# Summing the first adaLN gate on VectorE in column order, and holding the second gate's quarters back until the unsplit part of w_gate_up

## The chip, the core and the metric

The kernel runs on one core of a Trainium2 chip. A core has TensorE (PE in the profile; its weight loads are PEld), VectorE (DVE), ScalarE (ACT), GpSimd (POOL) and SyncE (SP), which here only issues the DMAs. The metric is the device time of one execution in microseconds (us). Before the change it is 1233.91 us, the median of three runs (1233.58 to 1235.08). All times below come from these runs or from one profiled execution of the same kernel.

## The reference, cut to what matters

One layer of a block over 256 tokens of width 2048, all in float32. What the change touches is the adaLN modulation: six vectors of 2048 values, made from one conditioning row `c` and a 2048 x 12288 matrix.

```python
mod = einsum('bd,de->be', silu(c), w_ada) + b_ada
shift1, scale1, gate1, shift2, scale2, gate2 = split(mod, 6)
h = rms_norm(x, norm1_w) * (1 + scale1) + shift1
proj = h @ w_in                      # 2048 x 6152
...                                  # mLSTM (4 heads) and differential attention (8 heads)
mix = concatenate([h_ml, o_da]) @ w_out
x = x + gate1 * mix
h = rms_norm(x, norm2_w) * (1 + scale2) + shift2
g, u = split(h @ w_gate_up, 2)       # 2048 x 11264
x = x + gate2 * ((silu(g) * u) @ w_down)
```

`gate1` is first needed when the first output columns of `w_out` are complete, `shift2` and `scale2` when the FFN's input is made, `gate2` only when the first output columns of `w_down` are complete.

## The kernel before

**The big products.** All four weight matrices are streamed once, in chunks of 128 x 1024 values. For each chunk ScalarE makes a rounded high half (`wh`, line 211) and VectorE the rest (`wl`, line 181); the activations exist in the same two halves (`hh`, `hl`, and others). TensorE then makes three products for each pair of column block and token half (lines 569 to 571), twelve products of 128 x 512 for one chunk. One chunk is a *tick*, and the kernel has 392 of them, written out in order by `visit`: the input projection in seven sweeps (ticks 0 to 95), the output projection (96 to 127, "wo"), the first twelve column groups of `w_gate_up` in three sweeps f0, f1, f2 over two, three and three of the eight column pairs of the input (128 to 223), its other ten groups in one piece (224 to 303, "fr"), and `w_down` (304 to 391, "dn"). f0 needs the column pairs 0 and 1 of the second scale and shift, f1 the pairs 2 to 4, f2 the pairs 5 to 7. The last two ticks of "wo" and the first two of f0 are split by token half; this is the turn.

**The modulation.** `w_ada` is loaded in 192 *quarters* of 128 x 1024 values (0.5 MB), eight eighths (p) of four quarters for each of the six vectors (s). The list `items` gives their order: the first scale and shift interleaved (64), the first gate (s = 2, 32), the second scale and shift interleaved (64), the second gate (s = 5, 32). A quarter is summed in one of two ways, told apart by `on_pe(s, p)`, which also picks its layout in memory (`_layout`):

- on TensorE: four matrix products with the activated `c` as weights (line 216; eight instructions in the profile) into a PSUM bank `gv`; after the fourth quarter ScalarE copies the row out (`gr`), TensorE turns it by two transposes into a second bank (`gc`, line 220), ScalarE copies that into `gsum`. A bank is held from the first of the four quarters on.
- on VectorE: one multiply with the activated `c` spread over the partitions (`silc`), with its sum written to `gsum` (line 185; two instructions in the profile).

`modcol` adds the partial sums of `gsum` and the bias on GpSimd (lines 377 and 379). For a gate, `gate_rows` does so once for all 16 columns, when all eight eighths are there, and then makes the gate's row in four pieces: VectorE spreads 512 values on a diagonal (`g1rd` for the first gate), TensorE multiplies by ones (`g1rp`), ScalarE copies. That is thirteen steps, at most one a half tick. `residual` multiplies the output columns by that row.

**What sets the order.** The program is written out half tick by half tick. A `Plan` keeps a running count of the work that waits on VectorE (`plan.v`), ScalarE (`plan.a`) and TensorE (`plan.p`), of the loads' landing times and of four free PSUM banks. In each half tick the loop at the end of `tile_block` emits the halves of the weights for two ticks ahead, then whatever small steps of attention, mLSTM, norm and gates are due (`plan.run`, in the order of a list, and only while `plan.v` and `plan.a` are at most 2.3 us), then the products. When a tick needs something that is not there yet, `plan.until` emits the steps of that alone, without products, until it is there.

Quarters are taken from the list, strictly in order, at two places. `due(i)` is a pace: as many quarters as `ADA_PLAN` has promised by tick i are taken at once, whatever else waits. `ada_idle` takes more when there is room: on TensorE while `plan.p` is at most 0.6 (and, at an eighth's first quarter, two banks are free), on VectorE while `plan.v` is at most 1.8, and only when the load should have landed. The ring of buffers `ada` holds four quarters; `ada_dma` issues the next load on SP's queue each time one is taken. SP issues in order, so a load that waits for its buffer holds up the weight loads behind it. Near the end of fr, the last two of the eleven FFN activation groups are written into the four buffers of this ring (`make_aT`, n of 9 and 10).

Of the kernel before, what the change touches and what calls it, by code (L numbers as in the profile page):

```python
# [27 lines left out]
NADA = 4  # L28
# [7 lines left out]


def on_pe(s, p):
    return (s == 1 and p % 3 != 2) or s == 2 or (s == 0 and p < PE0)


PE0 = 4
# [122 lines left out]
def tile_block(ctx, tc, x, c, pos, par, w_ada, w_in, w_gt, w_out, w_gu, w_dn, out):  # L165
# [85 lines left out]
    def load_x(cb, again=""):  # L251
        xs[cb] = slab(f"x{cb}{again}")
        nc.sync.dma_start(xs[cb].rearrange("p (t n) -> p t n", t=2), x_v[cb])
        plan.load(0.5)
# [45 lines left out]
    items = []  # L300
# [8 lines left out]
    ada_next = [0, 0]  # L309
    ada_ready = []  # L310

    def ada_dma(n=None):
        while ada_next[0] < len(items) and ada_next[0] < ada_next[1] + NADA and (n is None or n > 0):
            s, p, q = items[ada_next[0]]
            t = sl.tile([P, 1024], F32, name=f"ada{s}_{p}_{q}", tag="ada", bufs=NADA)
            nc.sync.dma_start(t[:], w_ada[s, p, q])
            ada_tiles[s, p, q] = t
            ada_ready.append(plan.load(0.5))
            ada_next[0] += 1
            n = None if n is None else n - 1  # L320

    def ada_use():
        s, p, q = items[ada_next[1]]
        t = ada_tiles.pop((s, p, q))
        if on_pe(s, p):
            if q == 0:
                assert plan.free > 0, "no bank"
                plan.free -= 1
                gemv[s, p] = misc(f"gv{s}_{p}")
            pg = gemv[s, p]  # L330
            for j in range(4):
                mm(pg[32 * j:32 * j + 32, :256], scol[:, q * 4 + j, :], t[:, j * 256:(j + 1) * 256], q == 0, q == 3,
                   passes=1.2, tile_position=(0, 32 * j))
            if q == 3:
                def finish():
                    yield 0
                    row = sm.tile([P, 256], F32, name=f"gr{s}_{p}", tag="gr", bufs=1)
                    act(row[:], pg[:, :256], AF.Copy)
                    plan.rel(1)
                    yield 1  # L340
                    pc = misc(f"gc{s}_{p}")
                    for j in range(2):
                        tr(pc[:, j * 128:(j + 1) * 128], row[:, j * 128:(j + 1) * 128])
                    yield 0
                    act(gsum[:, s, :, p * 2:p * 2 + 2],
                        pc[:, :256].rearrange("p (j a b) -> p a j b", j=2, b=32)[:, :, :, 0], AF.Copy)
                    plan.rel(1)
                w = Work(f"ada{s}_{p}", finish(), ())
                w.last = plan.now
                plan.works.insert(0, w)  # L350
        else:
            j, h = p * 2 + q // 2, q % 2
            stt(t[:], t[:], 1.0, silc[h][:], ALU.mult, ALU.mult, accum=gsum[:, s, h, j:j + 1])
            if q == 3:
                plan.mark(f"ada{s}_{p}")
        ada_next[1] += 1
# [152 lines left out]
    def weights_dma(limit=None):  # L509
        while state["dma"] < len(ticks) and state["live"] < NRAW and (limit is None or limit > 0):  # L510
            i = state["dma"]
            t = ticks[i]
            n = chunk_of[i][2]
            raw = wp.tile([P, 2048], F32, name=f"r{i}", tag="raw", bufs=NRAW)
            nc.sync.dma_start(raw[:, :n * 1024], t["src"][t["kb"]][:, t["h"] * 1024:(t["h"] + n) * 1024])
            raws[i] = raw
            raw_ready[i] = plan.load(n / 2)
            state["dma"] += n
            state["live"] += 1
            limit = None if limit is None else limit - 1  # L520

    def weights_hi(i):
        while state["hi"] <= min(i + HI_AHEAD, len(ticks) - 1):
            k = state["hi"]
            first, idx, n = chunk_of[k]
            if first not in raws:
                break
            plan.t = max(plan.t, raw_ready[first] - AHEAD * TICK)
            his[k] = wp.tile([P, 1024], F32R, name=f"wh{k}", tag="hi", bufs=NHL + HI_AHEAD)
            act(his[k][:], raws[first][:, idx * 1024:(idx + 1) * 1024], AF.Copy)  # L530
            state["hi"] += 1

    def weights_lo(i):
        while state["hl"] <= min(i, len(ticks) - 1):
            k = state["hl"]
            first, idx, n = chunk_of[k]
            raw = raws[first]
            hi = his.pop(k)
            lo = wp.tile([P, 1024], F32R, name=f"wl{k}", tag="lo", bufs=NHL)
            tt(lo[:], raw[:, idx * 1024:(idx + 1) * 1024], hi[:].bitcast(F32), ALU.subtract)  # L540
            wtiles[k] = (hi, lo)
            state["hl"] += 1
            if idx == n - 1:
                state["live"] -= 1
                del raws[first]
# [524 lines left out]
    def turn(stage, heads):  # L1070

        if stage == 0:
            residual_half(("wo", 3), rows1, 3, xs[3], 0)
            square_x(1, 3, 0, SQ0)
            finish_rms(1, 0)
            for p in range(2):
                next(heads[p, 0])
        elif stage == 1:
            plan.free -= 2
            for p in range(2):  # L1080
                next(heads[p, 0])
        elif stage == 2:
            residual_half(("wo", 3), rows1, 3, xs[3], 1)
            del accs["wo", 3], apart["wo", 3]
            plan.rel(1)
            next(heads[0, 0], None)
            square_x(1, 3, 1, SQ1)
            next(heads[1, 0], None)
            finish_rms(1, 1)
            for p in range(2):  # L1090
                next(heads[p, 1])
        elif stage == 3:
            plan.free -= 2
            for p in range(2):
                next(heads[p, 1])
        else:
            for p in range(2):
                next(heads[p, 1], None)
            plan.mark("norm2")
# [83 lines left out]
    spans = {}  # L1183
# [8 lines left out]
    for n, (groups, p0, p1) in enumerate(SWEEPS):  # L1192
        a = len(ticks)
# [4 lines left out]
    a = len(ticks)  # L1198
# [13 lines left out]
    for r, (p0, p1) in enumerate(FSWEEPS):  # L1212
        a = len(ticks)
# [10 lines left out]
    a = len(ticks)  # L1224
# [4 lines left out]
    a = len(ticks)  # L1229
# [12 lines left out]
    def load(span, n, margin):  # L1242
        a, b = spans[span]
        loads.append((a, max(b - margin, a + 1), n))

    for key, n, margin in ADA_PLAN:
        load(key, n, margin)

    def due(i):
        n = 8  # L1250
        for a, b, k in loads:
            n += k * min(max(i + 1 - a, 0), b - a) / (b - a)
        return min(int(n + 1e-6), len(items))


    plan.t = 3.2
    ada_dma(4)
    weights_dma(1)
    for cb in range(4):
# [5 lines left out]
    for n in range(4):  # L1265
        ada_use()
        ada_dma(1)
        if n < 3:
            next(h0)
# [68 lines left out]
    for i, t in enumerate(ticks):  # L1338
        plan.next_half()
        if i == turning + 1:  # L1340
            turn(4, heads)
        for fn in pending:
            fn()
        pending = []
        if i in (turning - 1, turning):
            turn((i - turning + 1) * 2, heads)
        weights_hi(i + AHEAD)
        weights_lo(i + (AHEAD if i == 0 or not LO_LATE or t["split"] is not None else AHEAD - 1))
        weights_dma()
        while ada_next[1] < due(i):  # L1350
            ada_use()
            ada_dma(1)
        ada_dma()
        if i == spans["wo"][0]:
            for cb in range(4):
                load_x(cb, "r")
        plan.run()
        if t["split"] is None:
            ada_idle()
        need = list(t["ready"])  # L1360
        if t["done"] and t["acc"][0] == "wo":
            need.append("rows1")
        plan.until(need, lambda: ada_idle(VFORCE))
        products(i, 0)
        plan.next_half()
        if i == turning - 2:
            weights_hi(turning + 1)
            weights_lo(turning + 1)
        elif t["split"] is None:
            weights_lo(i + AHEAD)  # L1370
            plan.run()
            ada_idle()
        products(i, 1)
        if i in (turning - 1, turning):
            turn((i - turning + 1) * 2 + 1, heads)
        pending += [fn for fn in (t["done"], t["mid"]) if fn]
# [17 lines left out]
        return next(self.gen)  # L1394


ADA_PLAN = ((0, 12, 3), (1, 16, 4), (2, 24, 3), (3, 4, 0), (4, 8, 0), (5, 8, 0), ("wo", 16, 22), ("f0", 24, 5), ("f1", 32, 5), ("f2", 32, 8))


def _layout(a):  # L1400
# [68 lines left out]
```

## Time and profile before

| | |
|---|---|
| median of three runs | 1233.91 us |
| the profiled execution | 1233.24 us |
| its span (first to last instruction) | 1231.5 us |
| granted TensorE clock, mean | 0.992 of full |
| quarters on TensorE / on VectorE | 72 / 120 |
| first gate's quarters (`gv` from 214 us on) | 214.9 to 339.7 us |
| quarters on VectorE, first and last | 54.6 and 707.9 us |

A row of a windows answer gives, for one stretch of the span, its length, then the busy time and number of instructions (x) of each engine in it, the granted TensorE clock, the mean busy share of the 16 DMA engines and their GB/s. With a tile's name it counts that tile's instructions alone. A row of a timeline gives start and duration in us, the engine, the line, the operation, the tile written and those read; in brackets the idle time ahead of it and what ended that. The records of consecutive matmuls overlap, since they are pipelined: what one costs is read from start to start.

### The profile page before, as it was taken

How to read it: one execution, taken by the hardware profiler on the slowest of the kernel's cores; microseconds unless marked ns; L12 is line 12 of the kernel's file. 1: busy time of each engine (PE TensorE's matmuls, PEld its weight loads, DVE VectorE, ACT ScalarE, POOL GpSimd, SP SyncE). 2: the span in 40 equal slices, each digit the busy share in tenths (PEclk: the TensorE clock that was granted, in tenths of full speed). 3: DMA queues.
4: the chain of work that ended last, by engine and by line, in shares of the span. 5: the costliest groups of instructions: out<-in, count | busy, mean ns of one | idle time of the engine just before them, and what ended most of it. 6: DMA issues, size and time to landing. Idle time of an engine off the chain costs nothing.

```text
span 1231.5 us, 15419 instructions
## 1 busy us (share of the span) xinstructions
PE 1208.9 (98%) x5842; PEld 956.2 (78%) x5842; DVE 815.3 (66%) x1064; ACT 587.1 (48%) x817; POOL 113.2 (9%) x250
## 2 busy tenths in 40 slices
PE   6999999999999999999999999999999999999998
PEld 2667878666778787788888888888888878888886
DVE  2656977577587998887988977445455454545443
ACT  3654454457566645855434544444444443343342
POOL 1010121210212412101100000000000000000000
PEclk8999999999999999999999999999999999999999
DMA  8879898757676898798999756555545545646471
GB/s 335 303 279 372 327 372 293 294 187 292 206 288 233 320 358 336 265 345 305 350 342 334 274 195 221 200 177 196 184 177 199 201 171 171 222 171 232 160 256 52
DMA packets 63260, 313.84 MB, mean 255 GB/s; under 512 B 6993, under 2 KB 7377, under 8 KB 41169
## 3 DMA queue, kind: packets, MB, share of 16 engines
q1 hardware_dynamic: 63186, 312.86, 70.1%
q8 instruction: 46, 0.75, 0.2%
q14 instruction: 28, 0.23, 0.1%
HBM read 310.73 MB, written 2.10 MB: 254 GB/s over the span
## 4 chain that ended last, share of the span: by engine, by line
PE 96%; DMA 1%; DVE 1%; ACT 1%; issue 0%; SPq 0%; POOL 0%; ACTq 0%
PE gv L216 3%; PE acc('dn', 0)_8036 L571 2%; PE acc('dn', 0)_8036 L569 2%; PE acc('dn', 2)_8838 L571 2%; PE acc('dn', 2)_8838 L570 2%; PE acc('dn', 1)_8458 L571 2%; PE acc('dn', 1)_8458 L570 2%; PE acc('dn', 0)_8036 L570 2%; PE acc('dn', 1)_8458 L569 2%; PE acc('dn', 2)_8838 L569 2%; DMA ada<-in_w_ada_dram 1%; PE apart('dn', 3)_9219 L571 1%; PE apart('dn', 3)_9219 L570 1%; PE acc('dn', 3)_9218 L571 1%; PE acc('dn', 3)_9218 L570 1%; PE apart('dn', 3)_9219 L569 1%
## 5 line engine op out<-in xcount | busy, mean ns | idle before, releaser
L181 DVE TENSOR_TENSOR wl<-r,wh 128x1024 fp32r<-128x1024 f32 x392 | 474.5, 1222 | 254.3 <-ACT wh L211 252.8
L211 ACT ACTIVATE wh<-r 128x1024 fp32r<-128x1024 f32 x392 | 410.3, 1058 | 409.6 <-DMA r<-in_w_gu_dram 62.1
L185 DVE SCALAR_TENSOR_TENSOR ada<-ada,silc 128x1024 f32<-128x1024 f32 x120 | 144.8, 1219 | 0.0
L377 POOL TENSOR_TENSOR modc<-part,gsum 128x2 f32<-128x2 f32 (+1 forms) x34 | 25.4, 747 | 395.1 <-DVE ada L185 277.5
L216 PE MATMUL gv<-ada,early 128*32 128x256 f32 x576 | 46.3, 416 | 4.3 <-DMA ada<-in_w_ada_dram 4.2
L216 PEld LDWEIGHTS gv<-ada,early 128*32 128x32 f32 x576 | 13.4, 112 | 29.4 <-issue 20.0
L569 PE MATMUL acc('dn', 0)_8036<-wh,aTh 128*128 128x512 f32 x88 | 35.9, 408 | 0.0
L379 POOL TENSOR_TENSOR modc<-modc,gsum 128x2 f32<-128x2 f32 (+1 forms) x58 | 30.9, 533 | 46.8 <-DVE ada L185 43.4
L571 PE MATMUL acc('dn', 0)_8036<-wh,aTl 128*128 128x512 f32 x88 | 34.3, 390 | 0.0
L570 PE MATMUL acc('dn', 0)_8036<-wl,aTh 128*128 128x512 f32 x88 | 34.3, 389 | 0.0
L569 PE MATMUL acc('dn', 1)_8458<-wh,aTh 128*128 128x512 f32 x88 | 34.2, 389 | 0.0
L570 PE MATMUL acc('dn', 1)_8458<-wl,aTh 128*128 128x512 f32 x88 | 34.2, 389 | 0.0
L571 PE MATMUL acc('dn', 1)_8458<-wh,aTl 128*128 128x512 f32 x88 | 34.2, 389 | 0.0
L569 PE MATMUL acc('dn', 2)_8838<-wh,aTh 128*128 128x512 f32 x88 | 34.2, 389 | 0.0
L570 PE MATMUL acc('dn', 2)_8838<-wl,aTh 128*128 128x512 f32 x88 | 34.2, 389 | 0.0
L571 PE MATMUL acc('dn', 2)_8838<-wh,aTl 128*128 128x512 f32 x88 | 34.2, 389 | 0.0
L181 DVE TENSOR_TENSOR hl<-hx,hh 128x512 fp32r<-128x512 f32 (+1 forms) x18 | 11.4, 632 | 26.5 <-ACT hh L211 26.2
L211 ACT ACTIVATE hx<-pt,modc,gcol 128x256 f32<-128x256 f32 (+1 forms) x36 | 17.4, 534 | 17.3 <-PE pt L220 11.5
L211 ACT ACTIVATE gr<-gv 128x256 f32<-128x256 f32 x18 | 6.9, 383 | 32.6 <-PE gv L216 32.6
L570 PEld LDWEIGHTS acc('dn', 0)_8036<-wl,aTh 128*128 128x128 f32 x88 | 16.5, 188 | 4.2 <-issue 1.0
L569 PEld LDWEIGHTS acc('dn', 0)_8036<-wh,aTh 128*128 128x128 f32 x88 | 16.5, 188 | 4.2 <-issue 1.0
L211 ACT ACTIVATE aTh<-at 128x512 fp32r<-128x512 f32 x22 | 11.9, 595 | 15.9 <-PE at L220 15.9
(987 smaller groups left out, 3019.0 us busy)
## 6 DMA issues: line engine op xcount, KB each, us to landing
ada<-in_w_ada_dram SPq DMA_DIRECT2D x192, 512.0 KB, 5.7
r<-in_w_gu_dram SPq DMA_DIRECT2D x76, 1024.0 KB, 5.0
r<-in_w_dn_dram SPq DMA_DIRECT2D x44, 1024.0 KB, 4.8
r<-in_w_in_dram SPq DMA_DIRECT2D x36, 1024.0 KB, 6.9
r<-in_w_out_dram SPq DMA_DIRECT2D x16, 1024.0 KB, 7.4
r<-in_w_in_dram SPq DMA_DIRECT2D x24, 512.0 KB, 5.9
r<-in_w_gu_dram SPq DMA_DIRECT2D x24, 512.0 KB, 5.3
x<-in_x_dram SPq DMA_DIRECT2D x4, 512.0 KB, 5.6
```

Of the source, the lines that this page charges most:

```text
L181: nc.vector.tensor_tensor(o, a, b, op=op)
L185: nc.vector.scalar_tensor_tensor(out=o, in0=a, scalar=s, in1=b, op0=op0, op1=op1, accum_out=accum)
L211: nc.scalar.activation(o, a, func, **kw)
L216: nc.tensor.matmul(o, l, r, start=start, stop=stop, **kw)
L377: nc.gpsimd.tensor_tensor(o, parts[0], parts[1], op=ALU.add)
L379: nc.gpsimd.tensor_tensor(o, o, y, op=ALU.add)
L569: nc.tensor.matmul(o, ah[:, s], wh[:, r], start=t["start"] and j == 0, stop=False)
L570: nc.tensor.matmul(o, ah[:, s], wl[:, r], start=False, stop=False)
L571: nc.tensor.matmul(o, al[:, s], wh[:, r], start=False, stop=t["stop"] and j == 1)
```

## The change

- The first gate's quarters are no longer TensorE's: `on_pe` is false for s = 2. They are laid out and summed like those of the second gate, on VectorE.
- No quarter of the second gate is loaded before the unsplit part of `w_gate_up` begins: `ada_dma` stops at `ada_limit`, 160 of the 192, until tick 224. The pace for f2 falls from 32 to 8 quarters, and from the fifth tick of fr on `due` asks for the last 32 in equal steps, up to 24 ticks ahead of its end.

```diff
 def on_pe(s, p):
-    return (s == 1 and p % 3 != 2) or s == 2 or (s == 0 and p < PE0)
+    return (s == 1 and p % 3 != 2) or (s == 0 and p < PE0)
...
+    ada_limit = [len(items) - 32]
+
     def ada_dma(n=None):
-        while ada_next[0] < len(items) and ada_next[0] < ada_next[1] + NADA and (n is None or n > 0):
+        while ada_next[0] < ada_limit[0] and ada_next[0] < ada_next[1] + NADA and (n is None or n > 0):
...
             n += k * min(max(i + 1 - a, 0), b - a) / (b - a)
+        a, b = spans["fr"]
+        if i >= a + 4:
+            n = len(items) - 32 + 32 * (i - 3 - a) / (b - 24 - a)
         return min(int(n + 1e-6), len(items))
...
         weights_dma()
+        if i == spans["fr"][0]:
+            ada_limit[0] = len(items)
+            ada_dma()
         while ada_next[1] < due(i):
...
-ADA_PLAN = (..., ("f1", 32, 5), ("f2", 32, 8))
+ADA_PLAN = (..., ("f1", 32, 5), ("f2", 8, 8))
```

More of the change, by code (lines that the diff above doesn't have):

```diff
@@ L1394, in __next__ @@
         return next(self.gen)
-ADA_PLAN = ((0, 12, 3), (1, 16, 4), (2, 24, 3), (3, 4, 0), (4, 8, 0), (5, 8, 0), ("wo", 16, 22), ("f0", 24, 5), ("f1", 32, 5), ("f2", 32, 8))
+ADA_PLAN = ((0, 12, 3), (1, 16, 4), (2, 24, 3), (3, 4, 0), (4, 8, 0), (5, 8, 0), ("wo", 16, 22), ("f0", 24, 5), ("f1", 32, 5), ("f2", 8, 8))
 def _layout(a):
```

## The prediction

> **What bounds the kernel now.** I read the page first: the span, the engines' totals, the slices and the chain that ended last.
>
> ```profile
> span 1231.5 us, 15419 instructions
> ...
> PE 1208.9 (98%) x5842; PEld 956.2 (78%) x5842; DVE 815.3 (66%) x1064; ACT 587.1 (48%) x817; POOL 113.2 (9%) x250
> ...
> DVE  2656977577587998887988977445455454545443
> ...
> PE 96%; DMA 1%; DVE 1%; ACT 1%; issue 0%; SPq 0%; POOL 0%; ACTq 0%
> ```
>
> The chain that sets the end is TensorE for 96% of its length. VectorE is busy for 66% on the whole, but unevenly: five to nine tenths in the first 23 slices, four to five tenths behind them. So the windows come next, cut where the projections begin: the input projection's last sweeps (206 to 391), the output projection (391 to 487), the three sweeps f0, f1, f2 over the split part of w_gate_up, and (from a second answer) its unsplit part fr.
>
> ```profile
> core 0: us, PE busy (x) PEld busy (x) DVE busy (x) ACT busy (x) POOL busy (x), PEclk, DMA share, GB/s
> 206.00:391.00 185.00, 185.00 (x1105) 137.22 (x1105) 132.65 (x266) 108.84 (x247) 34.23 (x99) 1.00 0.70 249
> 391.00:487.00 96.00, 95.34 (x431) 78.17 (x429) 88.98 (x127) 51.24 (x77) 27.43 (x41) 1.00 0.90 341
> 487.00:559.00 72.00, 69.06 (x313) 56.23 (x312) 57.58 (x80) 48.54 (x69) 7.58 (x12) 1.00 0.82 303
> 559.00:658.00 99.00, 99.00 (x442) 81.97 (x441) 87.14 (x106) 42.65 (x47) 9.97 (x10) 1.00 0.89 329
> 658.00:760.00 102.00, 102.00 (x471) 84.59 (x470) 84.06 (x90) 50.16 (x55) 2.65 (x4) 1.00 0.71 248
> ```
> ```profile
> 760.00:983.00 223.00, 223.00 (x1005) 184.98 (x1005) 109.85 (x96) 93.17 (x95) 0.00 (x0) 1.00 0.55 194
> ```
>
> TensorE has no gap anywhere but at the turn into the FFN (69.06 of 72). Work taken off it shortens its stretch unless something else becomes late; work moved between stretches in which it is never idle changes nothing. VectorE stands at 72% in 206:391, where the first gate is summed, and at 93% (88.98 of 96) right behind.
>
> **What leaves TensorE.** The first gate's 32 quarters are eight TensorE instructions each (`gv`), and each eighth of the gate ends in two transposes (`gc`). What one costs is read from the starts of its neighbours.
>
> ```profile
> 220.09 0.39 PE L570 MATMUL acc('in', 0, 4)_1821<-wl,hh 128*128 128x512 f32 x1
> 220.32 0.39 PE L571 MATMUL acc('in', 0, 4)_1821<-wh,hl 128*128 128x512 f32 x1
> 220.64 0.64 PE L216 MATMUL gv<-ada,early 128*32 128x256 f32 x8
> 221.21 0.50 PE L569 MATMUL acc('in', 0, 4)_1821<-wh,hh 128*128 128x512 f32 x1
> ...
> 233.42 0.40 PE L571 MATMUL acc('in', 2, 4)_1950<-wh,hl 128*128 128x512 f32 x1
> 233.74 1.07 PE L216 MATMUL gv<-ada,early 128*32 128x256 f32 x16
> 234.74 0.50 PE L569 MATMUL acc('in', 2, 4)_1950<-wh,hh 128*128 128x512 f32 x1
> ```
> ```profile
> 227.40 0.40 PE L571 MATMUL acc('in', 2, 4)_1950<-wh,hl 128*128 128x512 f32 x1
> 227.63 0.38 PE L220 MATMUL gc<-ident,gr 128*128 128x128 f32 x2
> 227.77 0.48 PE L569 MATMUL acc('in', 2, 4)_1950<-wh,hh 128*128 128x512 f32 x1
> ```
>
> Two products follow each other by 0.23 us (220.09, 220.32). Around one quarter it is 221.21 - 220.32 = 0.89, so the quarter costs 0.66; a pair costs 234.74 - 233.42 - 0.23 = 1.09; a pair of transposes 0.37 - 0.23 = 0.14, more where it stands alone among other transposes. In the timeline of `gv` half of the 32 stand alone (x8) and half in pairs (x16): 16 x 0.66 + 8 x 1.09 = 19.3, and 8 x 0.14 = 1.1: 20.4 us. The totals of the same tiles bound it from above:
>
> ```profile
> 206.00:391.00 185.00, 18.79 (x256) 5.86 (x256) 3.08 (x8) 1.00 0.70 249
> ```
> ```profile
> 206.00:391.00 185.00, 3.10 (x16) 2.17 (x16) 1.40 (x8) 1.00 0.70 249
> ```
>
> 18.79 + 3.10 = 21.9. I take **21 us** off TensorE, all of it in a stretch where nothing else was late: 206:391 would last 164. ScalarE loses 3.08 and the eight copies behind `gc`; it is at 59% there and not on the path: nothing. The eight banks for `gv` and eight for `gc` come free for attention, which I count at nothing.
>
> The Trainium skill speaks against reading it so: "Perfetto Trace Analysis", Identifying the Most-Contended Engine, says that a busy matmul row is no measure of TensorE's distance to its roofline, and takes the share of weight loads instead. By that rule the page's 78% would leave TensorE slack; the starts above, 0.23 apart without a break, say that in this stretch each instruction taken out closes up.
>
> **What VectorE gets.** One quarter there:
>
> ```profile
> 397.63 1.21 DVE L185 SCALAR_TENSOR_TENSOR ada<-ada,silc 128x1024 f32<-128x1024 f32 x1
> 398.77 0.07 DVE L185 DVE_READ_ACCUMULATOR ada<-ada,silc 128x1 f32 x1
> 398.77 1.21 DVE L185 SCALAR_TENSOR_TENSOR ada<-ada,silc 128x1024 f32<-128x1024 f32 x1
> ```
>
> From start to start 1.14 us, so 32 x 1.14 = 36.5 us. Whether they fit is a budget, and it needs VectorE's quarters of before, stretch by stretch (each is two instructions):
>
> ```profile
> 206.00:391.00 185.00, 11.50 (x20) 1.00 0.70 249
> 391.00:487.00 96.00, 32.53 (x54) 1.00 0.90 341
> 487.00:559.00 72.00, 22.57 (x37) 1.00 0.82 303
> 559.00:658.00 99.00, 34.60 (x58) 1.00 0.89 329
> ```
>
> About 9 quarters were done by 391, all of the second scale and shift; then 27, 18 and 29. Other VectorE work in 206:391 is 132.65 - 11.50 = 121.2. In the shortened 164 us at the 93% of the row behind it there is room for 152.5 - 121.2 = 31.3 us, 27 quarters. So of 41 (32 and those 9) some 14 slip into the output projection. There the rate cannot rise (93%), so the slip stays 14: the gate's last 5 come first, some 18 us in (5 of 27 in 96 us), and 22 of the second scale and shift by the turn, where 16 are needed. f0 was at 80% (57.58 of 72): 0.93 x 72 - 57.58 = 9.4 us, 8 quarters caught up. At f1's first ticks 40 are needed and 9 + 27 + 18 - 14 + 8 = 48 are there; at f2's 64 are needed and all are there. Each need is met, with 6 to 8 quarters to spare.
>
> What is queued behind the added quarters is VectorE's in-order list: the low halves of the weights, which TensorE needs within two ticks, and the steps of attention. The planner lets a quarter in only while its count of waiting VectorE work is at most 1.8 us, and the pace it must keep asks for only 16 of the 32 by the output projection. Two places are tight already.
>
> ```profile
> 397.71 2.53 DVE ada L185 x5
> ...
> 401.14 0.68 DVE odl L185
> ...
> 401.86 0.50 PE acc('wo', 0)_3635 L571
> ```
>
> At the output projection's start attention's last output comes from VectorE behind three quarters, and TensorE waits. If attention ends one tick later (12 products, 12 x 0.23 = 2.7 us) that is paid in full, for little other TensorE work is left there: **+2.7** (bounds 0, where the freed banks make up for it, to four ticks, 11).
>
> The other is the first gate's rows, needed when the first output columns end, 12 ticks (32 us) in:
>
> ```profile
> 348.94 1.19 POOL L377 TENSOR_TENSOR modc<-part,gsum 128x16 f32<-128x16 f32 x1
> 350.22 0.81 POOL L379 TENSOR_TENSOR modc<-modc,gsum 128x16 f32<-128x16 f32 x3
> ```
> ```profile
> L216 PE MATMUL g1rp<-g1rd,ones x8: 592/592/595, 374.8 to 408.7; 128*128 128x512 f32 x8
> L181 DVE TENSOR_TENSOR g1rd<-ident,modc x4: 677/683/684, 367.2 to 403.5; 128x512 f32<-128x512 f32 x4
> ```
>
> Before, the gate was summed by 348.94 and its rows were spread over 367 to 409. Now the last quarter falls 18 us into the stage; 14 us are left for 13 steps, one a half tick (17.7 us). So one or two of the four row pieces are made with TensorE waiting, each 0.68 on VectorE and 0.59 on TensorE: 2 x 1.27 = **+2.5** (bounds 0, and 4 x 1.27 plus GpSimd's 1.19 + 0.81: 7).
>
> **What is moved and costs nothing.** The second gate's 32 quarters leave f0 to f2, where TensorE shows no idle time but the 2.9 us at the turn, so nothing is gained. They land in fr with their 32 transfers of 0.5 MB on SP's queue; each waits there for the sum that frees its buffer, and the weight loads behind it wait too. The cover: VectorE has 109.85 of 223 us in fr, with 36.5 more 66%; the memory traffic was 194 GB/s, and even if the greedy filler takes the 32 in two thirds of fr (16.8 MB in 149 us, 113 GB/s more) that is about 307, below the 329 of 559:658, where 29 quarters went through in 99 us and TensorE was busy for all of them. Nothing, then; without that cover it would be a few us of late weights. The buffers are free again before the two last activations of the FFN, which take them over. The second gate's rows wait for the last activation anyway.
>
> **The sum.** 21 - 2.7 - 2.5 = 15.8. The profiled execution took 1233.24, 1.74 more than its span; so a span of 1215.7 and a run of 1217.4. The median of the three runs is 0.67 above the profiled one: **1218**.
>
> **The rivals.**
>
> A (forecast): as above; bounds of the unknown costs 0 to 18 of the 21.
>
> B: all 36.5 us of sums fit into VectorE's idle time and the freed banks bring attention forward. For it: 185 - 132.65 = 52 us idle in that stretch. Against it: 41 quarters by 391 need 121.2 + 46.7 = 168 of 164. It gives 1233.9 - 21 = 1213, or 1211 with a little at the turn.
>
> C: the slip grows beyond its reserve: the second scale and shift come late at the turn or at f1, and TensorE waits for quarters at 1.14 us each, with a transfer behind each. At 6 to 8 missing it costs 7 to 9 us beyond A's sum: 1226. For it: the reserve is only 6 to 8 quarters and the transfers in f0 and f1 already take 0.82 and 0.89 of the DMA engines. Against it: the reserve is positive at each of the three needs.
>
> D (slower): the quarters push attention's steps back, because its chain runs through the same in-order engine and the planner holds back steps at 2.3 us of waiting VectorE work, a mark that a quarter let in at 1.8 passes at once. From attention's end on TensorE waits in full: eight ticks late (8 x 2.7 = 21.6) use up the gain, nine make it slower. If VectorE keeps 26 of its 52 idle us (waits for TensorE and ScalarE inside the chain) and takes all 41 quarters first, the stretch lasts 132.65 + 36.5 + 26 = 195 instead of 185: 1244. Against it: the pace forces only 16 quarters there, 121.2 + 18.2 = 139 of 164 us.
>
> E: TensorE's freed time is taken up by waits that its dense row hides: no change, 1233. Against it stands the run of products 0.23 apart. It is where the rule of the Trainium skill's "Perfetto Trace Analysis" named above would lead.
>
> F: GpSimd becomes slow, and with it the reciprocal roots in attention.
>
> ```profile
> 368.01 1.06 POOL L389 TENSOR_TENSOR mfb<-mfb,mfx 128x4 f32<-128x4 f32 x1
> ...
> 369.44 0.20 POOL L391 TENSOR_TENSOR mf<-mf,mfb 128x4 f32<-128x4 f32 x1
> ```
>
> The same kind of operation takes 0.20 or 1.06, about one VectorE pass longer. A root is 12 such steps; if each met a quarter, 12 x 0.86 = 10 us would come on top ahead of the output projection, less the 2.7 counted: 1225. The Trainium skill, "SBUF — State Buffer", Who interferes with whom, gives this as a lock: a VectorE instruction with two SBUF inputs, as a quarter is, holds up a GpSimd instruction that reads SBUF. The trace agrees for a few of them; most steps of that root took 0.20 beside a busy VectorE.
>
> That the change does not do what it says: the second gate is not really paced evenly, since the filler takes quarters whenever there is room; it costs nothing either way.
>
> **How the numbers follow.** A 0.62, B 0.10, C 0.09, F 0.04, D 0.10, E 0.05. What a measurement of this kernel can tell from no change is about 0.2%, 2.5 us. A, B, C and F are faster: 0.85; E the same: 0.05; D slower: 0.10. The range 1211 to 1231 takes in A with its bounds (1213 to 1231), C, F and most of B; D, E and B's lower end, about 0.18, are left out.
>
> **What would show it.** No `gv` from 206 on; 152 quarters on VectorE instead of 120; the stretch from the first `acc('in', 0, 4)` to the end of the input projection at about 164 us; VectorE there above 90%; `g1rd` later than the start of the output projection; fr still 223 us with VectorE at two thirds; f0 to f2 unchanged in length. The prediction is wrong if TensorE shows idle time ahead of the output projection that adds up to more than some 10 us, or if a wait for `hh` or `hl` appears at the start of f1, or if fr grows.

## The result, and the profile after

The changed kernel takes 1241.1 us (median of four runs, 1240.32 to 1242.34) where the kernel before takes 1233.88: a ratio of 1.0058, 95% interval 1.004 to 1.0075. It is slower, by 7 us; 16 us of gain were forecast. The page of its profile:

```profile
span 1239.2 us, 14932 instructions
...
PE 1193.1 (96%) x5570; PEld 953.3 (77%) x5570; DVE 849.6 (69%) x1128; ACT 584.2 (47%) x801; POOL 118.4 (10%) x250
...
DVE  2656978799887998878855677878645454545453
...
PEclk8999999999997999999999999999999999999999
...
PE 85%; DVE 7%; POOL 2%; ACT 2%; issue 2%; DMA 1%; SPq 0%; DVEq 0%; ACTq 0%; POOLq 0%
```

TensorE is busy for 16 us less (the 21 us of the change, less some 5 us by which the rest got longer; more of this at the end), and is now 85% of the chain where it was 96%: VectorE, GpSimd and ScalarE have come onto it. In the 13th slice (372 to 403 us) the granted TensorE clock falls to 0.7. The windows, cut at the first product of each stage (last sweeps of the input projection; output projection; f0; fr), first after and then before at the same cuts:

```profile
207.20:365.50 158.30, 153.31 (x768) 124.38 (x767) 138.56 (x264) 94.27 (x189) 32.59 (x82) 0.99 0.63 227
365.50:496.20 130.70, 111.14 (x497) 88.37 (x495) 114.02 (x186) 64.07 (x122) 33.16 (x53) 0.93 0.86 318
496.20:566.70 70.50, 68.39 (x309) 55.99 (x310) 56.70 (x78) 47.11 (x65) 11.12 (x16) 1.00 0.78 289
...
768.40:990.60 222.20, 222.20 (x1002) 184.25 (x1002) 144.61 (x160) 93.20 (x95) 2.59 (x4) 1.00 0.72 269
```
```profile
207.00:391.70 184.70, 184.70 (x1104) 136.98 (x1103) 131.65 (x264) 109.54 (x249) 34.44 (x102) 1.00 0.70 249
391.70:489.80 98.10, 95.66 (x432) 78.02 (x430) 91.06 (x133) 52.09 (x79) 26.97 (x38) 1.00 0.91 345
```

The last sweeps of the input projection take 26.4 us less (158.3 against 184.7), and the output projection takes 32.6 us longer (130.7 against 98.1), with TensorE idle for 19.6 of it. The first is more than the 21 us because steps of attention and of the mLSTM slipped from one into the other: 65 TensorE instructions more than before stand in the output projection (497 against 432). f0 is a microsecond longer; f1, f2, fr and w_down are as long as before. So nearly all of the loss lies in these two stretches, and their sum is the number to follow below: **282.8 us before, 289.0 after, 261.8 if the 21 us had been gained**.

TensorE's waits in the changed kernel's output projection (who waited for whom: total us, times, longest):

```profile
PE ot L220 <- DVE o L181: 7.2, 1, 7.2
PE po L216 <- ACT aTs L211: 5.0, 3, 2.6
PE g1rp L216 <- DVE g1rd L181: 3.0, 1, 3.0
```

They are waits for attention's last heads (`ot`, `po`) and for the first gate's rows (`g1rp`). The chain that ended last, there:

```profile
366.08 2.08 ACT pm L211 x8
...
370.74 0.75 DVE pm L185 x2
371.49 1.14 DVE wl L181
372.62 1.07 DVE st L196 x4
...
373.83 1.06 POOL st L775
...
375.37 1.62 ACT pm L211 x7
...
377.42 0.95 PE po L216 x6
...
383.13 1.12 POOL of L390
...
387.39 1.22 DVE o L181
388.62 2.88 DVE ada L185 x5
...
392.05 0.67 DVE odl L185
392.77 0.79 PE acc('wo', 0)_3293 L573
```

Softmax (ScalarE), combination (`pm`), row maxima (`st`), scaling (GpSimd), softmax again, values, the root of the norm (GpSimd, twelve steps from 383.1 to 387.4), then nearly three microseconds of gate sums ahead of the low half (`odl`) for which the output product at 392.77 waits: one step after another. Beside the first of them TensorE still had output products, the last at 374.1 us; from there to 390.6 it had none, only attention's own small products and transposes. The order in which the program was written out says the same: at the third tick of the output projection, 13 half ticks were forced without products, and 8 more up to the twelfth tick; before there was one.

### The profile page after: what moved, and what is told of

The parts are those of the page before. It is cut to its first block, busy times and chain, and to the rows that moved or that the text cites. A ratio compares the mean times of both kernels' runs of the same rounds, so it can differ in the third digit from the quotient of the medians.

```text
span 1239.2 us, 14932 instructions
## 1 busy us (share of the span) xinstructions
PE 1193.1 (96%) x5570; PEld 953.3 (77%) x5570; DVE 849.6 (69%) x1128; ACT 584.2 (47%) x801; POOL 118.4 (10%) x250
## 4 chain that ended last, share of the span: by engine, by line
PE 85%; DVE 7%; POOL 2%; ACT 2%; issue 2%; DMA 1%; SPq 0%; DVEq 0%; ACTq 0%; POOLq 0%
DVE wl L181 2%; PE gv L216 2%; PE acc('dn', 0)_7884 L573 2%; PE acc('dn', 0)_7884 L572 2%; PE acc('dn', 2)_8686 L572 2%; PE acc('dn', 2)_8686 L571 2%; PE acc('dn', 1)_8306 L572 2%; PE acc('dn', 1)_8306 L571 2%; PE acc('dn', 0)_7884 L571 2%; PE acc('dn', 1)_8306 L573 2%; PE acc('dn', 2)_8686 L573 2%; DVE ada L185 1%; DMA ada<-in_w_ada_dram 1%; PE at L220 1%; PE apart('dn', 3)_9067 L572 1%
## 5 line engine op out<-in xcount | busy, mean ns | idle before, releaser
L185 DVE SCALAR_TENSOR_TENSOR ada<-ada,silc 128x1024 f32<-128x1024 f32 x152 | 183.4, 1219 | 1.0 <-DMA ada<-in_w_ada_dram 1.0
L571 PE MATMUL acc('dn', 0)_7884<-wh,aTh 128*128 128x512 f32 x88 | 35.9, 408 | 0.0
L573 PE MATMUL acc('dn', 0)_7884<-wh,aTl 128*128 128x512 f32 x88 | 34.3, 390 | 0.0
L572 PE MATMUL acc('dn', 0)_7884<-wl,aTh 128*128 128x512 f32 x88 | 34.3, 389 | 0.0
L571 PE MATMUL acc('dn', 1)_8306<-wh,aTh 128*128 128x512 f32 x88 | 34.2, 389 | 0.0
L572 PE MATMUL acc('dn', 1)_8306<-wl,aTh 128*128 128x512 f32 x88 | 34.2, 389 | 0.0
L573 PE MATMUL acc('dn', 1)_8306<-wh,aTl 128*128 128x512 f32 x88 | 34.2, 389 | 0.0
L571 PE MATMUL acc('dn', 2)_8686<-wh,aTh 128*128 128x512 f32 x88 | 34.2, 389 | 0.0
L572 PE MATMUL acc('dn', 2)_8686<-wl,aTh 128*128 128x512 f32 x88 | 34.2, 389 | 0.0
L573 PE MATMUL acc('dn', 2)_8686<-wh,aTl 128*128 128x512 f32 x88 | 34.2, 389 | 0.0
```

Of the source, the lines that this page charges most:

```text
L185: nc.vector.scalar_tensor_tensor(out=o, in0=a, scalar=s, in1=b, op0=op0, op1=op1, accum_out=accum)
L571: nc.tensor.matmul(o, ah[:, s], wh[:, r], start=t["start"] and j == 0, stop=False)
L572: nc.tensor.matmul(o, ah[:, s], wl[:, r], start=False, stop=False)
L573: nc.tensor.matmul(o, al[:, s], wh[:, r], start=False, stop=t["stop"] and j == 1)
```

## The experiments

The theories. **1, order:** without TensorE's quarters the planner's half ticks are shorter, its count of VectorE work decays less in each, and attention's steps are held back at its mark until they stand bare. **2, VectorE's time:** it cannot take 36.5 us more there. **4, the hold** of the second gate costs. **5, the chain:** attention's steps run through five engines and need their time; TensorE's quarters were work beside them, and without them TensorE waits. Theory 5 came up after the first four runs (there was no theory 3). "Stretch" is the sum of the two stretches above, in the profiled execution; "short" sums, products and roots do part of the work and leave the result incomplete or less exact. Each ratio is against the kernel before on the same chip.

| run | us | ratio, 95% interval | stretch |
|---|---|---|---|
| e1 first gate alone | 1244.05 | 1.0075 (1.006 to 1.009) | 288.9 |
| e2 hold alone | 1234.17 | 0.9998 (0.9989 to 1.0008) | 282.9 |
| e3 short sums | 1231.45 | 0.9978 (0.9968 to 0.9988) | 279.5 |
| e4 mark at 3.4 | 1243.35 | 1.0067 (1.0052 to 1.0082) | 289.3 |
| e5 first gate free | 1238.33 | 1.0023 (1.0008 to 1.0038) | 283.8 |
| e6 short sums, mark | 1234.29 | 0.9995 (0.9985 to 1.0005) | 278.8 |
| e7 before, mark | 1243.5 | 1.0074 (1.0059 to 1.0089) | 286.4 |
| e8 two eighths, mark | 1242.69 | 1.0063 (1.0048 to 1.0078) | 285.9 |
| e9 order of before | 1244.56 | 1.0076 (1.0062 to 1.009) | 292.8 |
| e10 short products | 1225.91 | 0.993 (0.9916 to 0.9943) | 275.1 |
| e11 summed twice | 1252.32 | 1.0145 (1.0131 to 1.0159) | 300.4 |
| e12 order of before, short sums | 1227.74 | 0.9943 (0.993 to 0.9957) | 276.0 |
| e13 two eighths | 1234.4 | 0.9999 (0.999 to 1.0008) | 281.4 |
| e14 four eighths | 1240.05 | 1.0044 (1.0032 to 1.0057) | 290.2 |
| e15 as e12, short roots | 1218.19 | 0.986 (0.9844 to 0.9877) | 265.6 |
| e16 before, short roots | 1233.73 | 0.9993 (0.9983 to 1.0002) | 282.8 |
| e17 change, short roots | 1233.06 | 0.9988 (0.9979 to 0.9997) | 278.9 |
| e18 two eighths, short roots | 1230.29 | 0.9966 (0.9952 to 0.9979) | 278.9 |

**Which half of the change.** e1 leaves out the hold, e2 keeps the first gate on TensorE.

```diff
-    return (s == 1 and p % 3 != 2) or (s == 0 and p < PE0)                # e2 only
+    return (s == 1 and p % 3 != 2) or (s == 0 and p < PE0) or s == 2
```

> Part one alone: the first gate on VectorE, the second gate's quarters where they were before. If the loss comes from the first gate alone (theory 1 and 2), this takes what the changed kernel takes, 1239 to 1243 us. If holding the second gate back costs anything (theory 4: its quarters in fr, or the empty ring in f2), this is faster than the changed kernel by that much, below 1238.

> Part two alone: the first gate stays on TensorE, the second gate waits for fr. Theory 1 and 2 (the loss is the first gate's) expect no difference from before, 1232 to 1236 us, since f0 to fr have no TensorE gaps either way. Theory 4 (the hold costs) expects 1238 or more.

The first gate alone has the whole loss, the hold alone does nothing: theory 4 falls. (With the first gate on VectorE and no hold, f2 took 105.5 us in the profile against 102.9 with it, so there the hold may be worth a little; the intervals of e1 and of the change overlap.)

**The same order with less VectorE work, and a later mark.** e3 sums 64 of 1024 values and counts the full cost; e4 only raises the mark.

```diff
-            stt(t[:], t[:], 1.0, silc[h][:], ..., accum=...)
+            w = 64 if s == 2 else 1024                                     # e3
+            stt(t[:, :w], t[:, :w], 1.0, silc[h][:, :w], ..., accum=...)
+            plan.v += (1024 - w) / 960
...
-VMAX = AMAX = 2.3
+VMAX, AMAX = 3.4, 2.3                                                      # e4
```

> The changed kernel with the same program order, but each of the first gate's 32 sums runs over 64 of the 1024 values, so that gate is left incomplete; the planner still counts the full cost. VectorE loses about 32 x 1.0 = 32 us of work. Theory 1 (the planner's order: attention's steps held back by its mark for waiting VectorE work, then made at the output projection's start with no products beside them) expects most of the loss to stay: 1230 to 1240 us, only the quarters inside the forced steps being saved. Theory 2 (VectorE has too much work in that stretch) expects the 21 us off TensorE to show: 1210 to 1217.

> The changed kernel with the planner's mark for VectorE's waiting work, above which no step of attention is emitted, at 3.4 us instead of 2.3; all work is the same. By the planner's own list attention then ends earlier: 4 forced half ticks ahead of the third tick of the output projection instead of 13, and 5 more for the gate's rows instead of 8. Theory 1 expects most of the loss back and some gain: 1217 to 1229 us. Theory 2 expects no change beyond 3 us: 1238 to 1243, since VectorE has the same work in the same time.

e3 came to the lower edge of what theory 1 said: 9.5 us of the stretch go with VectorE's work, but 17.7 of the 21 stay lost without it. Against theory 1, e4 gained nothing (1243 is the upper end of what theory 2 expected): the waits left the output projection (111.4) and came up in the input projection (177.9). So neither theory alone would do, and theory 5 was set against both.

**Nothing counted, nothing paid; and the mark's control.** e5 counts 0 for the short sums; e6 is e3 with the mark of e4; e7 is the kernel before with that mark; e8 puts only the last two eighths on VectorE, with it.

```diff
-            plan.v += (1024 - w) / 960
+            plan.v -= w / 960 + 0.07 if s == 2 else 0                      # e5
```

> The first gate's sums run over 64 of 1024 values (the gate is left incomplete), and the planner counts 0 for them: the first gate's quarters cost neither TensorE nor VectorE anything, and nothing is held back for them. What is left is attention's own chain of steps in an input projection that is 21 us shorter. Theory 2 (VectorE's added time) expects the full 21 us: 1211 to 1216. Theory 5 (attention's chain runs through five engines and needs its time; TensorE's quarters were its cover, so without them the output projection waits) expects less than half of that: 1223 to 1232, with the waits at the start of the output projection still there; the planner's own list has 13 forced half ticks in it, against 1 before and 21 in the changed kernel.

> Both at once: sums over 64 of 1024 values (gate incomplete, full cost counted) and the mark at 3.4. The order is that of the kernel with the mark at 3.4 alone (1243), VectorE has 32 us less. If that kernel's new waits inside the input projection are VectorE's time, they go: 1212 to 1220. If they are attention's chain itself (theory 5), most stay: 1228 to 1238.

> A control: the kernel before with the mark at 3.4. The planner's list has no forced half tick, one fewer than before. If the higher mark by itself makes TensorE wait for late low halves, this is slower than before by some us, 1237 to 1243; if it is harmless, 1231 to 1235.

> The change for the last two of the gate's eight eighths alone (8 quarters on VectorE, 24 stay on TensorE), mark at 3.4, second gate held back. TensorE loses 8 x 0.66 = 5 us, VectorE gets 9; the planner's list has no forced half tick. Theory 5 expects a gain of up to 5 us, 1229 to 1234, since the cover is still there; if the mark alone costs, it is slower than before by what the control shows.

e5 is a miss for theory 2 and further than theory 5 went: with a first gate that costs neither engine anything, the kernel is still slower than before. It is not clean, though: the second scale and shift moved up into the free room. The control spoils e4, e6 and e8 as measures of order: the mark alone costs the kernel before 9 us, in its profiled execution mostly in f0 and f2 (4.7 and 4.6 us longer, against 3.6 in the stretch). e8 takes what the control takes. These three are inconclusive but for one difference: e6 against e4, one order with and without the sums, is 9 us in time. e6's 1234 lies where theory 5 expected it (1228 to 1238), yet the mark is in it.

**One order for all.** So the order of before was kept in the changed kernel: each quarter of the first gate is summed on VectorE, but admitted and counted as TensorE's.

```diff
+        if s == 2:                                                         # e9
+            stt(t[:], t[:], 1.0, silc[h][:], ..., accum=gsum[:, s, h, j:j + 1])
+            plan.v -= 1024 / 960 + 0.07
+            plan.p += 4 * 1.2 * 256 / 2400
...                                       # and the banks and steps of the row, counted only
-            if on_pe(s, p):
+            if on_pe(s, p) or s == 2:                                      # in ada_idle
```

e10 and e11 are the kernel before with one side of the change each: 16 of 256 columns in three of four quarters' products (e10), or a second, unread sum of each of those quarters on VectorE (e11).

> The change with the program order of before: the first gate is summed on VectorE and the second one is held back, but the planner takes and counts each of the first gate's quarters as if it still ran on TensorE (0.51 us of TensorE, a bank held, nothing on VectorE). Every step of attention then stands at the half tick where it stood before. If the loss is the program order (theory 1, by the shorter half ticks of the plan), the gain shows: 1213 to 1224 us. If attention's chain needs its time and TensorE's quarters were its cover (theory 5), or VectorE has too much work (theory 2), TensorE waits at other places instead: 1230 to 1243.

> TensorE's part alone, in the order of before: the first gate's quarters stay on TensorE, but three of each four multiply 16 of their 256 columns (the gate is left incomplete), counted in full. TensorE loses 24 quarters of about 0.43 us of streaming, some 8 to 10 us; VectorE gets nothing. Theory 1 and 2 expect all of it: 1224 to 1227. Theory 5 expects less than half: 1230 to 1234.

> VectorE's part alone, in the order of before: the first gate stays on TensorE and each of its quarters is also summed on VectorE, in two halves, into a place nobody reads, not counted by the planner; VectorE gets 32 x 1.3 = 42 us. Theory 2 expects VectorE to become late: 1240 or more. Theory 1 and 5 expect its idle time to take it: 1233 to 1237.

Their last sweeps of the input projection, e9, e10, e11 (the output projection is 98.1 in all three):

```profile
207.90:402.60 194.70, 171.90 (x833) 138.75 (x832) 167.21 (x328) 106.00 (x233) 38.59 (x102) 0.92 0.67 237
```
```profile
208.00:385.00 177.00, 175.90 (x1105) 135.88 (x1104) 131.35 (x264) 109.18 (x249) 34.53 (x102) 1.00 0.71 262
```
```profile
207.10:409.40 202.30, 189.40 (x1104) 139.11 (x1104) 173.35 (x392) 109.54 (x249) 37.56 (x102) 0.98 0.66 228
```

Theory 1 falls as the cause: with every step where it stood, the loss is larger, and the waits only sit elsewhere. e10 pays nearly in full, 7.7 us of stretch for 8.8 us less of TensorE (175.90 against 184.70). That is what theories 1 and 2 expected; theory 5, which expected less than half, missed it. Of the 1.1 us missing, 1.0 is a wait of TensorE for the normalized k. And e11 shows VectorE's time as a price, against theories 1 and 5: 41.7 us more of it (173.35 against 131.65) make the stretch 17.6 longer, with the same products in the same order. TensorE's waits in e11 are 10.8 us for q, k and v, 1.6 for an mLSTM head, and none for the low halves of the weights. In both kernels that overload VectorE it is busy for 86% of the stretch (167.21 of 194.70, 173.35 of 202.30). The next expectations take this for a possible ceiling. It is none: the changed kernel stands at 88% there (138.56 of 158.30), and with shorter roots (e17, below) at 91% (138.41 of 151.80).

**What is left without VectorE's time, and the price by eighths.** e12 is e9 with sums over 64 values; e13 and e14 are e9 with p in (0, 1) and in (0, 2, 4, 6) on VectorE.

> The kernel that keeps the order of before (1244.6), but each of the first gate's sums runs over 64 of 1024 values (that gate is left incomplete). TensorE is rid of its 21 us, VectorE gets next to nothing, the order is that of before. Theory 2 (VectorE's time is what is missing) expects the whole gain: 1211 to 1216. If attention's chain itself needed TensorE's quarters as cover (theory 5), 1225 or more.

> The order of before, the first two of the gate's eight eighths on VectorE, six on TensorE. TensorE loses 8 x 0.66 = 5.3 us, VectorE gets 8 x 1.14 = 9.1, where it was busy for 58% (207 to 246). If VectorE has a ceiling near the 86% at which it stood in the two kernels that overload it, it is far below it here and nearly all of the gain shows: 1228 to 1231. If each us on VectorE costs TensorE the 0.42 us that the kernel summed twice shows on average: -5.3 + 3.8, 1232 to 1234.

> The order of before, every other eighth on VectorE: 16 quarters, 18.2 us on VectorE, 10.6 us off TensorE. With a ceiling at 86% of the input projection's last sweeps, 131.7 + 18.2 = 150 of 174 us is just at it: 1223 to 1229. At 0.42 us per us: -10.6 + 7.7, 1230 to 1233. If VectorE's waits lie in the same places as attention's, slower than before: 1235 or more.

e12's stretch, and what TensorE waited for in it:

```profile
208.00:385.90 177.90, 166.75 (x833) 135.62 (x833) 135.63 (x328) 105.70 (x233) 34.24 (x102) 0.96 0.71 260
```
```profile
PE po L216 <- DVE proj L181: 4.0, 1, 4.0
PE tpk L220 <- DVE proj L181: 3.5, 1, 3.5
PE tpq L220 <- DVE proj L181: 3.4, 2, 2.5
```

Theory 2 alone is out: its 1211 to 1216 is far from 1227.7, which lies where theory 5 expected it (1225 or more). Only 6.8 us of stretch came back of 21, and TensorE is idle for 11.2, waiting for the normalized q and k and for v. (VectorE still has 4.0 us more than before here, the 32 short sums, so not all of the missing 14 need be the chain.) Between e12 and e9, in one order, lie 31.6 us of VectorE (167.21 - 135.63) and 16.8 of stretch. e13 gains nothing, and e14 loses 7.4 us of stretch, as only its third expectation had it: VectorE's microseconds have a price well below 86%, too (e14 stands at 149.49 of 192.10, 78%). At e11's average of 0.42 the 17.8 us that e14 puts on VectorE would have cost 7.5, less than the 10.6 it takes off TensorE; so more comes on top: the chain, which e14 uncovers as well, and 2.6 us in which TensorE waits for the load of a quarter. How much each has is not taken apart.

**The chain, shortened.** In the normalization of q and k, and at attention's and the mLSTM's ends, GpSimd refines a reciprocal root in three steps of four instructions. One step instead of three makes the roots less exact and changes neither TensorE's nor VectorE's work, nor the order:

```diff
-        for _ in range(3):
+        for _ in range(1):
             nc.gpsimd.tensor_tensor(b, y, y, op=ALU.mult)
```

e15 is e12 with it, e16 the kernel before, e17 the changed kernel, e18 is e13.

> The kernel with the order of before and short sums of the first gate (1227.7), in which TensorE waits some 11 us for transposes of q and k, with one refinement step instead of three in each reciprocal root on GpSimd (8 GpSimd instructions fewer per root; the roots are inexact). The order, TensorE's and VectorE's work are unchanged. If attention's chain sets the stretch now (theory 5), each of the four roots of q and k ends 2.2 to 4 us earlier and the waits shrink: 1219 to 1225. If the waits come from VectorE's list alone, no change: 1226 to 1229.

> The control: the kernel before with the same shortened roots. There TensorE has no wait in that stretch, so the chain's length does not matter: 1232 to 1235.

> The changed kernel with one refinement step instead of three in each root on GpSimd (less exact roots). The shortened chain is worth 9.6 us where VectorE is relieved; here VectorE still has its 36.5 us, and the chain stands bare at the output projection's start, where one root of attention and one of the mLSTM lie on it (2.2 us each at least). Theory 5 with theory 2: 1233 to 1238, still not faster than before. Theory 5 alone: 1220 to 1230.

> Two of eight eighths on VectorE in the order of before, with the shortened roots. Without them this kernel took what before took, with 4.3 us of TensorE idle in the last sweeps of the input projection. If those waits are the chain, most of them go: 1229 to 1232, faster than both kernels. If they are VectorE's time: 1233 to 1235.

e15's stretch:

```profile
207.50:375.00 167.50, 162.71 (x833) 132.10 (x832) 135.61 (x328) 105.63 (x233) 20.39 (x51) 0.99 0.75 276
```

With VectorE's 135.6 unchanged, 10.4 us are gone (177.9 to 167.5), more than expected; TensorE's idle time falls from 11.2 to 4.8, and its products run at a granted clock of 0.99 instead of 0.96. In the kernel before the same edit changes nothing that can be measured. That is theory 5, beside theory 2: the chain was hidden behind TensorE's work, and came out when 21 us of that work went. In the changed kernel's own order short sums give back 9.5 us of stretch (e3) and short roots 10.1 (e17); both at once were not run in that order, so 7.6 of the 27.2 us lost there are not taken apart. With the chain shorter the change is just level with before (e17, 8 us better than without), and two eighths on VectorE beat both kernels (e18: 1230.29, 0.3% under before, with the less exact roots).

## Why the prediction was wrong, point by point

**What holds.** No `gv` after 206 us, 152 quarters on VectorE, fr at 222.2 us with VectorE at 65% (144.61 of 222.20) and memory at 269 GB/s, f1 and f2 as long as before: the parts "costs nothing" hold, and e2 shows them alone. Nothing came late at the turn, f1 or f2 to speak of (f0 is 1 us longer). TensorE's 21 us were well sized: in e15's stretch, where the clock is 0.99, it is busy for 22.0 us less than before (162.71 against 184.70).

**"I take 21 us off TensorE, all of it in a stretch where nothing else was late."** This is the step that failed first. That TensorE had no gap showed only that everything else was in time, not how much earlier it was. e12 measures what could be had: 7 us; after that the chain of q, k and attention is the bound, and of the other 14 the roots on GpSimd alone account for 10 (e15). In the profile of before this stands nowhere as a wait, but it can be read: from the end of the VectorE instruction that finishes a tile to the start of the TensorE instruction that reads it. These are the rows for the first q, the first k and the first v:

```profile
229.86 0.50 DVE L181 TENSOR_TENSOR proj<-rpq 128x128 f32<-128x128 f32 x2
230.63 0.38 PE L220 MATMUL tpq<-ident,proj 128*128 128x128 f32 x2
...
249.93 0.49 DVE L181 TENSOR_TENSOR proj<-rpk 128x128 f32<-128x128 f32 x2
250.57 0.30 PE L220 MATMUL tpk<-ident,proj 128*128 128x128 f32 x1
...
319.71 1.22 DVE L181 TENSOR_TENSOR proj<-proj,acc('in', 4, 4)_2691 128x1024 f32<-128x1024 f32 x1 [1.23 <-PE acc('in', 4, 4)_2691 L571]
322.10 0.38 PE L216 MATMUL po<-proj,aTs 128*128 128x128 f32 x2
```

TensorE came only 0.3, 0.15 and 1.2 us after them (and 3.1 after the second q). In e12 it waits at the same places, for 0.9, 3.5 and 4.0 us (and 2.5).

**"At the 93% of the row behind it there is room."** The room was there, or nearly: VectorE reached 88% in that stretch, and 91% with shorter roots. But 22 quarters instead of 27 were done by its end (44 instructions of `ada` in the changed kernel's windows, the same 44 in e17's shorter stretch: the planner's order sets this number), so 19 slipped instead of 14. And the budget asked whether the work fits, when the question was what each microsecond of it does to the steps behind it in the same list. Its price in one order is 16.8 us of stretch for 31.6 of VectorE, below that rate as well (e14).

**"One tick later ... +2.7 (bounds 0 ... to four ticks, 11)."** The output projection got 32.6 longer. The direction was right, the size was not: the bound was four ticks, where 13 half ticks without products stood at the third tick alone. And the idle time that the prediction named as its sign of being wrong, ahead of the output projection, was only 5.0 us there (158.30 - 153.31): it lies inside the output projection.

**The gate's rows, +2.5.** TensorE waited 3.0 us for them (`g1rp`): right in size, though in part by luck, since the gate's last sum began 29 us into the output projection (394.4) and not 18.

**Rival D, at 0.10,** was what happened as to place (attention's end, at the start of the output projection) and sign; its price was 10 us, the time shows 7. Its point against itself, that the pace forces only 16 quarters, did not help: the kernel in which the gate's sums are next to nothing and are not counted (e5) waits too. Of its two mechanisms VectorE's in-order list is about half of what is lost along one order (e9 against e12); the planner's mark was only where the loss appears: with the old order (e9) it appears in the input projection and is larger.

**Rival E, at 0.05,** had the other mechanism: waits that TensorE's dense row hides. Such waits took up 14 of the 21 us in e12, and in the changed kernel, with VectorE's time, more than all. What was held against it, products 0.23 apart without a break, is the reading that failed.

**Rival F** had the right engine, but for another reason: the roots were not slower. Most GpSimd steps took 0.20 us as it says (some 1.1, as the `of` step in the chain above); they matter at that length, as they stand one behind another.

In sum, along one order: -21 hoped for; +14 by the chain behind TensorE (e12, with 4 us of short sums on VectorE); +17 by VectorE's time (e9): 10 us longer. With the planner's own order after the change it is 6 (289.0 against 292.8). VectorE's price is paid mostly through attention's steps: from e12 to e9 the waits for q, k and v grew from 10.9 to 18.5 us, those for low halves only to 2.1. What stays open: why short sums give back 16.8 in one order and 9.5 in the other. No other value of the mark was tried.

## What to carry to other kernels

An engine without gaps says that the others are in time, not by how much: before work is taken off it, read how far behind it the next chain runs, from the end of each tile's last write to the start of its first use on that engine. Or take the work away in the same order without putting it anywhere else, which here gave 7 of 21 (e12); taking only a part of it away (e10) would have looked like full pay. Room on an engine is not enough: price added work by what stands behind it in the same list. A chain of small dependent steps on a hardly used engine (GpSimd was busy for 9%) can be the next bound.

## What the runs showed of the hardware

TensorE pays for waits twice. These are rows of the changed kernel's windows (TensorE alone: length, busy time, instructions, granted clock, DMA), and of its chain between the second and the third:

```profile
374.00:377.40 3.40, 0.83 (x6) 1.00 1.05 416
380.00:381.70 1.70, 1.58 (x6) 0.50 0.95 311
398.00:402.00 4.00, 4.00 (x22) 1.00 0.28 76
```
```profile
393.56 0.43 PE acc('wo', 0)_3293 L571
393.99 0.43 PE acc('wo', 0)_3293 L572
```

The granted clock is at half by 380 us, behind waits of 2.6 and 1.2 us and already ahead of the wait of 7.2 us (from 381.6 on), and back at full in 398:402, though TensorE has work again from 388.8 on. Products follow each other by 0.43 us in between, against 0.23 elsewhere. The mean granted clock is 0.93 in that output projection and 0.92 in e9's input projection, where it was 1.00 before. The Trainium skill, "TensorE: Matmul & The Clock Gate", What's actually happening, has the idle state at half clock, from an idle window of about 3.4 us on; the trace agrees in the factor (0.50). Over the two stretches TensorE's idle time grew by 22 us and its busy time fell by only 16 (264.45 against 280.36) where 21 were taken out: by this estimate some 5 of the 27 us lost are products at the lower clock.

In one kernel the mark of 3.4 us instead of 2.3 for VectorE's waiting work cost 9 us (e7), though the program's list looked better by it, with no forced half tick.
